# Two-layer hybrid trunk, float32: score matmuls over two PSUM tags, the 32x32 inverses laid out by Vector-engine transposes, output tiles in another pool tag, the second first-layer norm from bn_stats

## Chip, cores and metric

One core of a Trainium2 chip runs the whole program. The metric is device time in microseconds (us) of one execution. The median of three runs of the kernel before is 2872.01 us (2871.85 to 2873.32).

## The reference

256 tokens of width 2048 go through two layers. Each layer normalises the input, multiplies it with one large input projection, runs four token mixers (A to D), projects and gates their outputs, and adds a normalised output projection. Everything is float32. In the code, `ya` is the gated linear attention of `pa`, `yb` the top-k attention of `pb`, `yc` the delta-rule recurrence of `pc` and `yd` the gated token mixer of `pd`.

```python
for l in range(DEPTH):
    h = _rmsnorm(x, norm_pre[l])
    p = h @ w_in[l]
    pa, pb, pc, pd, pm = _split(p, GROUP_COLS)
...
    ys = jnp.stack([ya, yb, yc, yd], axis=2).astype(x.dtype)
    proj = jnp.einsum('bsgw,gwd->bsgd', ys, w_proj[l])
    gates = jax.nn.sigmoid(pm.reshape(bsz, seq, N_BRANCH, D_MODEL).astype(F32))
    merged = jnp.einsum('bsgd,bsgd->bsd', gates, proj.astype(F32)).astype(x.dtype)
    x = x + _rmsnorm(merged @ w_out[l], norm_post[l])
```

The change touches mostly branch C. Its recurrence, per head of 64 channels (16 heads):

```python
def step(state, inp):
    r_t, w_t, k_t, v_t, kk_t, a_t = inp
    sa = jnp.einsum('bhvk,bhk->bhv', state, -kk_t)
    state = (state * w_t[:, :, None, :]
             + sa[..., None] * (kk_t * a_t)[:, :, None, :]
             + v_t[..., None] * k_t[:, :, None, :])
    return state, jnp.einsum('bhvk,bhk->bhv', state, r_t)
```

The kernel computes it in chunks of 64 tokens. Within a chunk it needs the scores between all pairs of tokens (tile `pG`) and the inverse of a unit triangular 64x64 matrix for each head and chunk (tile `TT`), put together from two 32x32 inverses and the block between them.

## The kernel before

**Weights.** `weights` streams the projection matrices with 1 MB DMAs on the SyncE queue (`raw`). Each 128x512 piece is split into a high part `wh` by ScalarE (ACT) and a rest `wl` by VectorE (DVE), three buffers of each. TensorE (PE) makes three products for each piece: high x high, rest x high, high x rest. `product` puts tokens on the PSUM partitions (`mm`, 512 columns wide), `product_cm` puts channels there (`mc`, 256 columns), `product_both` does half of each (`mb`). `shift` is the column at which a split piece starts in its 576-column buffer: 16 by default, 56 in `d_mixer`.

**Stages of a layer.** `pre` transposes the normalised input (`trT`) and splits it into `xT`, ACT the high part and DVE the rest. `small` makes the 280 narrow columns. `c_pair` runs eight times, once for two heads, with the projection of the next pair beside it. `c_solve` makes the inverses, `c_chain` carries the state over four chunks, with `b_index` and `b_pair` (branch B) interleaved. Then come `merge(2)`, branch A, `merge(1)`, `d_mixer`, `merge(0)`, `merge(3)` and `finish`, which makes the layer's output `x` and the next layer's normalised input `o`.

**Order.** A framework schedules the instructions when the program is built, and puts each engine's into a fixed order; an engine runs its own in that order and waits on semaphores. `high_priority` moves instructions ahead in it. Buffers come from pools by tag. A tag with n buffers makes the n+1st tile wait for the readers of the first. PSUM has three tags: `mm` with four banks, `mx` (method `pm`) and `mc` (method `pc`) with two each. The product tiles named `mc` and `mb` lie in tag `mm`.

**Pair scores.** In `c_pair` the two score tiles `pG` come from `pc`, and each is filled by four 64-row matmuls from `kb` and `AR`. GpSimd (POOL) makes `ks` from `kb`, which PE transposes into `pkt`. `pv` transposes the values for `VU`, whose unused half POOL sets to zero in `c_begin`.

**Solve.** `c_solve` runs a forward substitution on DVE in 62 operations on `slv` (128 partitions are 128 blocks of 32x32). The result `X` is written to a DRAM buffer `d2` (shown as `d`), and read back by four DMAs on ACT's queue into `TT`, which has heads and block rows on the partitions. DVE transposes the low blocks of `TT` into `slv` (L645), and PE makes `pzt` and `pet` from them, 64 matmuls of 32x32 each.

**Slots.** `c8` holds six tiles of 16 KB a partition, among them `AR`, `KT`, `VU`, `m2` and `o`. `tt` holds one tile, either `TT` or `npost` (the gain of the output norm). POOL clears a quarter of `TT` twice a layer (L634). The inverse square roots of all norms are a power on POOL (L183).

Of the kernel before, what the change touches and what calls it, by code (L numbers as in the profile page):

```python
# [24 lines left out]
KT = DM // 128  # L25
# [103 lines left out]
class Trunk:  # L129
    def __init__(self, ctx, tc, ins, out, depth=DEPTH, dbg=None):  # L130
        self.ctx, self.tc, self.nc, self.i, self.out, self.depth = ctx, tc, tc.nc, ins, out, depth
        self.dbg = dbg
        self.sb = ctx.enter_context(tc.tile_pool(name="sb", bufs=1))
        self.ps = ctx.enter_context(tc.tile_pool(name="ps", bufs=4, space=PSUM))
        self.dr = ctx.enter_context(tc.tile_pool(name="dr", bufs=1, space=DRAM))
        self.off = 0
        self.BUFS = {"s8": 2, "c8": 6, "tt": 1, "ev": 2, "t2": 8, "s1": 5, "xT": 16, "Y": 2, "c1": 2, "bs": 2, "SP": 2, "zz": 3}

# [226 lines left out]

    def norm(self, x, h):

        ss = self.one([128, 4], "ss", bufs=2)
        for c in range(4):
            junk = self.t("t2", [128, 512], "junk")  # L370
            self.act(junk, x[:, c * 512:(c + 1) * 512], AF.Square, accum_out=ss[:, c:c + 1])
        s1 = self.one([128, 1], "ss1", bufs=2)
        self.nc.vector.tensor_reduce(s1, ss, AX.X, OP.add)
        self.rsqrt(s1, s1, 1.0 / DM, EPS)
        for c in range(4):
            if c % 2:
                self.act(h[:, c], x[:, c * 512:(c + 1) * 512], scale=s1)
            else:
                self.ts(h[:, c], x[:, c * 512:(c + 1) * 512], s1, OP.mult)

    def pre(self, H):

        xT = [self.t("xT", [128, 2, 256], "xT", F32R) for _ in range(KT)]
        for t in range(2):
            for j in range(0, KT, 4):
                ps = self.pm([128, 4, 128], "trT")
                for b in range(4):
                    self.tr(ps[:, b, :], H[t][:, j // 4, b * 128:(b + 1) * 128])
                for b in range(4):
                    s = self.pcol[:, j + b:j + b + 1]  # L390
                    hi, lo = (xT[j + b][:, a, t * 128:(t + 1) * 128] for a in range(2))
                    self.act(hi, ps[:, b, :], scale=s)
                    self.stt(lo, ps[:, b, :], s, hi.bitcast(F32), OP.mult, OP.subtract)
        return xT

    def layer(self, l, H, src):
        nc, i = self.nc, self.i
        self.pcol = self.one([128, NPCOL], "pcol", bufs=2)
        nc.scalar.dma_start(self.pcol, i["pcol"][l])
        self.l = l  # L400
        self.xT = self.pre(H)
        if l == 0:
            self.rope_tables()
        self.small()
        self.c_begin()
        for p in range(8):
            self.c_pair(p)
        self.c_solve()
        ys = {g: [] for g in range(4)}
        self.c_chain(ys[2])  # L410
        self.b_index()
        for p in range(4):
            self.b_pair(p, ys[1])
        self.m2 = [self.t("c8", [128, DM], "m2") for _ in range(2)]
# [26 lines left out]
    def small(self):  # L441
        nc, l = self.nc, self.l
        pa = self.product(self.xT, KT, 280, range(9), range(9))
        s = self.t("ev", [128, 2, 280], "small")
        for t in range(2):
# [50 lines left out]
    def c_pair(self, p):  # L496
# [73 lines left out]
        G = self.t("Y", [128, 2, 4, 128], "G")  # L570
        pg = [self.pc([128, 4, 2, 64], "pG") for _ in range(2)]
        for s in range(4):
# [24 lines left out]
    def c_begin(self):  # L597
        self.AR, self.KT, self.VU, self.bsd = [], [], [], []
        for g in range(2):
            self.AR.append(self.t("c8", [128, 4, 4, 2, 64], "AR"))  # L600
            self.KT.append(self.t("c8", [128, 4, 4, 128], "KT"))
            vu = self.t("c8", [128, 4, 4, 128], "VU")
            self.nc.gpsimd.memset(vu[64:128, :, 0:4:2, :], 0.0)
# [6 lines left out]
    def c_solve(self):  # L610
# [14 lines left out]
        for j in range(31):  # L625
# [3 lines left out]
            self.tt(X[:, 0:j + 1, j + 1:32], X[:, 0:j + 1, j + 1:32], o, OP.add)  # L629
        d2 = self.dr.tile([2, 2, 32, 32, 32], F32, name="d2", bufs=2)  # L630
        nc.scalar.dma_start(d2.rearrange("a b q j t -> (a b q) j t"), X)
        TT = self.t("tt", [128, 32, 64], "TT")
        for h in range(2):
            nc.gpsimd.memset(TT[h * 64 + 32:h * 64 + 64, :, 0:32], 0.0)  # L634
            for qp in range(2):
                r = 64 if qp == 0 else 0
                nc.scalar.dma_start(TT[h * 64:h * 64 + 32, qp * 16:qp * 16 + 16, 32:64],
                                    Gd[r:r + 32, qp * 16:qp * 16 + 16, 0, h * 64 + 32:h * 64 + 64])
            for b in range(2):
                g = h * 64 + b * 32  # L640
                nc.scalar.dma_start(TT[g:g + 32, :, b * 32:(b + 1) * 32], d2[h, b].rearrange("q j t -> j q t"))

        TA, Z = X, M
        for h in range(2):
            nc.vector.transpose(TA[h * 64:h * 64 + 32], TT[h * 64:h * 64 + 32, :, 0:32])  # L645
        lo, hi = ([slice(h * 64 + o, h * 64 + o + 32) for h in range(2)] for o in (0, 32))
# [288 lines left out]
    def d_mixer(self, ys):  # L935
# [25 lines left out]
        for b in range(2):  # L961
            pa = self.product_cm(self.xT, KT, 512, 56)
            u = self.t("ev", [128, 4, 256], "du")
            for j in range(2):
                self.act(u[:, 2 * j:2 * j + 2, :], pa[j], AF.Gelu)
            for j in range(2):
# [8 lines left out]
                self.tt(o, o, w.rearrange("p g t i -> p g (t i)"), OP.mult)  # L975
            pa = self.product_cm(self.xT, KT, 512, 56)
            self.y_slots(ys, 4 * b)
# [34 lines left out]
    def finish(self, src, last):  # L1012
        nc, l = self.nc, self.l
        X = self.load_x(src)
        npost = self.t("tt", [128, DM], "npost")
        nc.scalar.dma_start(npost, self.i["rows"][l, 2304:4352].partition_broadcast(128))
        ss, s1 = [self.one([128, 4], f"osum{t}") for t in range(2)], []
        o = [self.t("c8", [128, 4, 512], "o") for _ in range(2)]
        for d in range(4):
            pa = self.product(self.mT, KT, 512, *((range(8, KT), range(5, KT)) if d == 3 else ()))  # L1020
            for t in range(2):
                junk = self.t("t2", [128, 512], "junk")
                self.act(junk, pa[t], AF.Square, accum_out=ss[t][:, d:d + 1])
                self.tt(o[t][:, d], pa[t], npost[:, d * 512:(d + 1) * 512], OP.mult)
                if d == 3:
# [15 lines left out]
    def run(self):  # L1041
        src = self.i["x"]
        X = self.load_x(src)
        H = [x.rearrange("p (d c) -> p d c", d=4) for x in X]
        self.consts()
        for t in range(2):
            self.norm(X[t], H[t])
        for l in range(self.depth):
# [30 lines left out]
```

## Time and profile before

| | kernel before |
|---|---|
| median of 3 runs | 2872.01 us (2871.85 to 2873.32) |
| profiled execution | 2873.88 us |
| its span in the trace | 2872.1 us |
| PE busy | 2821.7 us (98%) |
| DVE, ACT, POOL busy | 1821.6 (63%), 1484.8 (52%), 174.6 us (6%) |
| mean granted PE clock | 0.995 of full |
| HBM traffic | 185 GB/s over the span |

Busy shares of PE are of pipelined matmuls, whose ends are modelled: a matmul of 128x512 is shown with 0.39 us although the next starts 0.23 us later. So times on PE are read from start to start. The 40-slice view of the page has PE at 9 tenths everywhere but in the first slice and the last. The granted clock reads 1.00 at 2.4 GHz and 0.50 at 1.2 GHz.

### The profile page before, as it was taken

Reading aid. Unit: us, or ns where it says so; the run is one execution under the profiler, and the core shown is the slowest. Engines: PE = TensorE matmul, PEld = TensorE weight load, DVE = VectorE, ACT = ScalarE, POOL = GpSimd, SP = SyncE. Lnnn points to the kernel's source line nnn. Section 1 sums busy time; section 2 is a strip of 40 time slices with the busy share of each in tenths; the row PEclk is TensorE's granted clock in tenths of the full one; section 3 lists DMA queues with packets and bytes.
Section 4 is the critical chain, followed back from the end, with each engine's and each line's share of the span. In section 5 each row is a group of like instructions: output and inputs, shape, how many; then the busy total and the mean of one; then the engine's idle time right before and its main releaser. Section 6 shows DMA issues by size and latency. Waiting matters only on the chain.

```text
span 2872.1 us, 44940 instructions
## 1 busy us (share of the span) xinstructions
PE 2821.7 (98%) x17264; PEld 2442.0 (85%) x17264; DVE 1821.6 (63%) x3319; ACT 1484.8 (52%) x2674; POOL 174.6 (6%) x263
## 2 busy tenths in 40 slices
PE   7999999999999999999989999999999999999998
PEld 6999888887778898888889988898877888988886
DVE  6777857555555655656567779575555556555565
ACT  6455555545444545445565545555554544544454
POOL 1222001000000000000022120110000000000000
PEclk9999999999999999999999999999999999999999
DMA  5555656555455555555555556565545555555554
GB/s 183 182 180 188 192 165 204 179 191 184 166 178 191 189 209 192 191 197 183 184 181 179 181 185 194 158 208 188 197 165 174 183 191 199 197 193 196 191 184 160
DMA packets 100799, 533.56 MB, mean 186 GB/s; under 512 B 30852, under 2 KB 31108, under 8 KB 40742
## 3 DMA queue, kind: packets, MB, share of 16 engines
q1 hardware_dynamic: 68256, 486.96, 48.9%
q10 hardware_dynamic: 26568, 24.85, 3.2%
q0 software_dynamic: 5760, 18.88, 2.0%
q8 instruction: 135, 2.21, 0.3%
q14 instruction: 80, 0.66, 0.1%
HBM read 512.83 MB, written 17.83 MB: 185 GB/s over the span
## 4 chain that ended last, share of the span: by engine, by line
PE 78%; issue 16%; DMA 2%; DVE 2%; ACT 1%; POOL 0%; ACTq 0%; DVEq 0%; POOLq 0%
PE mm L169 49%; PE mc L169 16%; PE mb L169 6%; PE pG L169 1%; DVE wl L157 1%; DMA bs<-bsd 1%; PE pkv L169 1%; PE pW L169 1%; PE pao L169 0%; PE trT L173 0%; PE pY L169 0%; DMA d<-slv 0%; DMA TT<-d 0%; ACT wh L154 0%; PE psc L169 0%
## 5 line engine op out<-in xcount | busy, mean ns | idle before, releaser
L157 DVE TENSOR_TENSOR wl<-raw,wh 128x512 fp32r<-128x512 f32 (+1 forms) x1822 | 1250.4, 689 | 888.6 <-ACT wh L154 884.2
L154 ACT ACTIVATE wh<-raw 128x512 fp32r<-128x512 f32 (+1 forms) x1822 | 1145.7, 630 | 1198.0 <-DVE wl L157 598.3
L169 PE MATMUL mm<-wh,xT 128*128 128x512 f32 (+1 forms) x4216 | 1327.2, 391 | 0.9 <-ACT wh L154 0.9
L169 PEld LDWEIGHTS mm<-wh,xT 128*128 128x128 f32 x4216 | 784.7, 188 | 166.6 <-ACT wh L154 4.8
L169 PE MATMUL mm<-wl,xT 128*128 128x512 f32 (+1 forms) x2108 | 826.9, 392 | 2.7 <-DVE wl L157 2.6
L169 PE MATMUL mc<-xT,wh 128*128 128x256 f32 x3072 | 532.0, 282 | 0.0
L169 PEld LDWEIGHTS mm<-wl,xT 128*128 128x128 f32 x2108 | 395.7, 188 | 92.1 <-DVE wl L157 9.1
L169 PEld LDWEIGHTS mc<-xT,wh 128*128 128x128 f32 x3072 | 447.7, 188 | 5.1
L169 PE MATMUL mc<-xT,wl 128*128 128x256 f32 x1536 | 384.3, 285 | 1.5 <-DVE wl L157 0.9
L169 PE MATMUL mm<-wh,yT 128*128 128x512 f32 x1024 | 321.0, 389 | 0.0
L169 PEld LDWEIGHTS mc<-xT,wl 128*128 128x128 f32 x1536 | 266.0, 188 | 4.9 <-DVE wl L157 3.9
L169 PEld LDWEIGHTS mm<-wh,yT 128*128 128x128 f32 x1024 | 192.1, 188 | 41.3 <-ACT aex L154 1.5
L169 PE MATMUL mm<-wl,yT 128*128 128x512 f32 x512 | 199.4, 389 | 0.0
L169 PE MATMUL mb<-wh,xT 128*128 128x256 f32 x512 | 120.3, 288 | 3.8 <-ACT wh L154 3.8
L169 PEld LDWEIGHTS mm<-wl,yT 128*128 128x128 f32 x512 | 96.1, 188 | 19.9
L169 PE MATMUL mb<-xT,wh 128*128 128x256 f32 x512 | 103.0, 285 | 0.0
L169 PEld LDWEIGHTS mb<-wh,xT 128*128 128x128 f32 x512 | 89.1, 192 | 6.7 <-ACT wh L154 4.2
L169 PEld LDWEIGHTS mb<-xT,wh 128*128 128x128 f32 x512 | 80.1, 192 | 0.8 <-issue 0.5
L169 PE MATMUL mb<-wl,xT 128*128 128x256 f32 x256 | 75.2, 294 | 0.4 <-DVE wl L157 0.4
L169 PE MATMUL mb<-xT,wl 128*128 128x256 f32 x256 | 72.9, 285 | 0.0
L169 PE MATMUL mm<-wown,xT 128*128 128x280 f32 (+1 forms) x204 | 50.0, 387 | 8.1 <-ACT xT L154 5.3
L183 POOL TENSOR_TENSOR orsq<-orsq,mhalf 128x1 f32<-128x1 f32 x4 | 2.4, 588 | 881.0 <-DVE orsq L163 880.9
(280 smaller groups left out, 1924.8 us busy)
## 6 DMA issues: line engine op xcount, KB each, us to landing
raw<-in_w_dram SPq DMA_DIRECT2D x456, 1024.0 KB, 4.8
Gd<-G POOLq DMA_DIRECT2D x32, 256.0 KB, 3.0
Gq<-Gd ACTq DMA_DIRECT2D x8, 1024.0 KB, 5.2
raw<-in_w_dram SPq DMA_DIRECT2D x8, 560.0 KB, 4.0
bsd<-bs POOLq DMA_DIRECT2D x16, 256.0 KB, 4.4
bs<-bsd POOLq DMA_DIRECT2D x16, 256.0 KB, 3.7
x<-in_x_dram ACTq DMA_DIRECT2D x4, 512.0 KB, 5.9
x<-in_x_dram SPq DMA_DIRECT2D x4, 512.0 KB, 7.2
```

Of the source, the lines that this page charges most:

```text
L154: self.nc.scalar.activation(out, in_, f, **kw)
L157: (eng or self.nc.vector).tensor_tensor(out, a, b, op)
L169: self.nc.tensor.matmul(out, lhsT, rhs, start=start, stop=stop, **kw)
L183: self.nc.gpsimd.tensor_tensor(out, out, self.mhalf[:, :n], OP.pow)
```

## The change

- **Pair scores:** one of a pair's two `pG` tiles comes from `pc` and one from `pm`, so that they lie in different PSUM tags.
- **Solve:** DVE transposes `X` twice, straight after the substitution: into `TA` (the scratch tile `slvt`) and into `TT[:, :, 0:32]`, with transposed strides. ACT copies the high blocks from there to `TT[:, :, 32:64]`, and POOL clears their old place afterwards. The DRAM buffer, its write and its four reads are gone.
- **Slots:** `c8` has four buffers, a new tag `vu` has two, for `VU`, `m2` and `o`. `npost` becomes two tiles of 1024 columns in tag `Y`, so `tt` holds `TT` alone.
- **Start:** a 1-element activation (`warm`) stands before the constants. The two norms of the first layer have high priority, and the one of the second token half takes its mean square from `bn_stats` on DVE, not from ACT's squares. The hi and lo splits of `pre` have high priority, and `rope_tables` is called after the product of `small`.
- **d_mixer:** `product_cm` uses the default shift 16 for 56.

```diff
-        self.BUFS = {"s8": 2, "c8": 6, "tt": 1, "ev": 2, "t2": 8, "s1": 5, "xT": 16, "Y": 2, "c1": 2, "bs": 2, "SP": 2, "zz": 3}
+        self.BUFS = {"s8": 2, "c8": 4, "vu": 2, "tt": 1, "ev": 2, "t2": 8, "s1": 5, "xT": 16, "Y": 2, "c1": 2, "bs": 2, "SP": 2, "zz": 3}
...
-    def norm(self, x, h):
+    def norm(self, x, h, stats=False):
...
+        if stats:
+            st, mv = self.t("c1", [128, 4, 6], "nst"), self.t("s1", [128, 2], "nmv")
+            for c in range(4):
+                self.nc.vector.bn_stats(st[:, c, :], x[:, c * 512:(c + 1) * 512])
+            self.nc.vector.bn_aggr(mv, st.rearrange("p b s -> p (b s)"))
+            self.stt(s1, mv[:, 0:1], mv[:, 0:1], mv[:, 1:2], OP.mult, OP.add)
+            self.rsqrt(s1, s1, 1.0, EPS)
...
                 ps = self.pm([128, 4, 128], "trT")
+                with self.tc.high_priority():
...
-        if l == 0:
-            self.rope_tables()
         self.small()
...
-        pg = [self.pc([128, 4, 2, 64], "pG") for _ in range(2)]
+        pg = [f([128, 4, 2, 64], "pG") for f in (self.pc, self.pm)]
...
-            vu = self.t("c8", [128, 4, 4, 128], "VU")
+            vu = self.t("vu", [128, 4, 4, 128], "VU")
...
-        d2 = self.dr.tile([2, 2, 32, 32, 32], F32, name="d2", bufs=2)
-        nc.scalar.dma_start(d2.rearrange("a b q j t -> (a b q) j t"), X)
-        TT = self.t("tt", [128, 32, 64], "TT")
+        TT, TA, Z = self.t("tt", [128, 32, 64], "TT"), tmp, M
+        nc.vector.transpose(TA.rearrange("p q j -> p j q"), X)
+        nc.vector.transpose(TT[:, :, 0:32].rearrange("p q t -> p t q"), X.rearrange("p j t -> p t j"))
         for h in range(2):
-            nc.gpsimd.memset(TT[h * 64 + 32:h * 64 + 64, :, 0:32], 0.0)
+            s = slice(h * 64 + 32, h * 64 + 64)
+            self.act(TT[s, :, 32:64], TT[s, :, 0:32])
+            nc.gpsimd.memset(TT[s, :, 0:32], 0.0)
...
-            for b in range(2):
-                g = h * 64 + b * 32
-                nc.scalar.dma_start(TT[g:g + 32, :, b * 32:(b + 1) * 32], d2[h, b].rearrange("q j t -> j q t"))
-        TA, Z = X, M
-        for h in range(2):
-            nc.vector.transpose(TA[h * 64:h * 64 + 32], TT[h * 64:h * 64 + 32, :, 0:32])
...
-            pa = self.product_cm(self.xT, KT, 512, 56)
+            pa = self.product_cm(self.xT, KT, 512)
...
-        npost = self.t("tt", [128, DM], "npost")
+            npost.append(self.t("Y", [128, 1024], "npost"))
-        o = [self.t("c8", [128, 4, 512], "o") for _ in range(2)]
+        o = [self.t("vu", [128, 4, 512], "o") for _ in range(2)]
...
+        warm = self.t("s1", [128, 1], "warm")
+        self.nc.gpsimd.memset(warm, 0.0)
+        self.act(warm, warm, AF.Square)
...
-            self.norm(X[t], H[t])
+            with self.tc.high_priority():
+                self.norm(X[t], H[t], t == 1)
```

How the built order moves, at three places. On PE, the scores of the first pair of layer 0, in the kernel before (`mc` are products of the next pair):

```order
L169 MATMUL pG<-AR,kb 128x128 x4
L169 MATMUL mc_835<-xT,wh 128x256
L169 MATMUL mc_835<-xT,wl 128x256
L169 MATMUL mc_835<-xT,wh 128x256 x2
L169 MATMUL mc_835<-xT,wl 128x256
L169 MATMUL mc_836<-xT,wh 128x256
L169 MATMUL pG<-AR,kb 128x128 x4
```

and in the changed kernel:

```order
L169 MATMUL mc_836<-xT,wl 128x256
L169 MATMUL pG<-AR,kb 128x128 x8
L173 MATMUL pkt<-cst,ks 128x128 x4
L173 MATMUL pv<-cst,cm 128x128 x2
L169 MATMUL mc_837<-xT,wl 128x256
```

Two groups of four scores with products between them have become one group of eight, with `pkt` and `pv` right behind it.

On DVE, the first transposes after the substitution in layer 0, in the kernel before (`qk` belongs to branch B; the last operation of the substitution stands nine rows ahead of the first transpose):

```order
L157 TENSOR_TENSOR wl<-raw,wh 128x512
L157 TENSOR_TENSOR qk<-ropet 128x8x16 x2
L645 STREAM_TRANSPOSE slv<-TT 32x1024
L157 TENSOR_TENSOR wl<-raw,wh 128x512 x2
L645 STREAM_TRANSPOSE slv<-TT 32x1024
L157 TENSOR_TENSOR wl<-raw,wh 128x512 x6
```

and in the changed kernel:

```order
L157 TENSOR_TENSOR slv<-slv,slvt 128x31
L641 STREAM_TRANSPOSE slvt<-slv 128x32x32
L642 STREAM_TRANSPOSE TT<-slv 128x32x32
L157 TENSOR_TENSOR wl<-raw,wh 128x512 x3
L166 SCALAR_TENSOR_TENSOR by<-po,bg 128x512
```

The two transposes stand right behind the substitution, ahead of the next three splits.

On POOL, the change of layers, in the kernel before (`orsq` and `ss` are inverse roots of norms, `xs` is the output of a layer going to DRAM):

```order
L1035 DMA xs<-x_13545 128x512 x4
L603 MEMSET VU 64x8x128
L604 MEMSET VU 64x8x128
L634 MEMSET TT 32x32x32 x2
L183 TENSOR_TENSOR orsq<-orsq,mhalf 128x1
L183 TENSOR_TENSOR ss_14275<-ss_14275,mhalf 128x1
```

and in the changed kernel:

```order
L183 TENSOR_TENSOR orsq<-orsq,mhalf 128x1
L1043 DMA xs<-x_13542 128x512 x4
L183 TENSOR_TENSOR orsq<-orsq,mhalf 128x1
L183 TENSOR_TENSOR ss_14265<-ss_14265,mhalf 128x1
L1043 DMA xs<-x_13545 128x512 x4
```

The four memsets no longer stand between the layer's output and the two inverse roots.

## Rows read from the trace of the kernel before

**Rows 1.** The page: PE's busy time, and DVE's split group (count, busy us, mean ns).

```profile
PE 2821.7 (98%) x17264; PEld 2442.0 (85%) x17264; DVE 1821.6 (63%) x3319; ACT 1484.8 (52%) x2674; POOL 174.6 (6%) x263
...
L157 DVE TENSOR_TENSOR wl<-raw,wh 128x512 fp32r<-128x512 f32 (+1 forms) x1822 | 1250.4, 689 | 888.6 <-ACT wh L154 884.2
```

**Rows 2.** Timeline of PE around one score group: start us, duration us, operation, count.

```profile
200.41 0.28 PE L169 MATMUL mc<-xT,wh 128*128 128x256 f32 x1
200.61 1.16 PE L169 MATMUL pG<-AR,kb 64*128 64x128 f32 x8
201.70 0.38 PE L169 MATMUL mc<-xT,wh 128*128 128x256 f32 x1
201.92 0.29 PE L169 MATMUL mc<-xT,wl 128*128 128x256 f32 x1
```

**Rows 3.** The tile `ks` in the same pair, instructions that write it.

```profile
L584 POOL TENSOR_TENSOR ks<-kb,P x1: 1431/1431/1431, 198.1 to 198.1; 128x512 f32<-128x512 f32 x1
```

**Rows 4.** Timeline of DVE after the substitution in layer 0.

```profile
361.29 0.21 DVE L157 TENSOR_TENSOR slv<-slv,slvt 128x31 f32<-128x31 f32 x1
...
374.48 1.23 DVE L645 STREAM_TRANSPOSE slv<-TT 32x1024 f32<-32x1024 f32 x1 [6.25 <-DMA TT<-d]
```

**Rows 5.** Timeline of ACT and its queue, same stretch.

```profile
367.89 5.06 ACTq L641 DMA_DIRECT2D TT<-d  x3
373.08 0.63 ACT L154 ACTIVATE wh<-raw 128x512 fp32r<-128x512 f32 x1 [5.97 <-issue]
```

**Rows 6.** Timeline of PE, same stretch, then two groups by form over the span.

```profile
364.90 0.36 PE L169 MATMUL mb<-wh,xT 128*128 128x256 f32 x1
...
370.64 1.03 PE L173 MATMUL pqk<-cst,qk 128*128 128x128 f32 x8
373.76 0.39 PE L169 MATMUL mb<-wh,xT 128*128 128x256 f32 x1 [2.09 <-ACT wh L154]
...
375.77 0.42 PE L169 MATMUL pzt<-slv,TT 32*32 32x32 f32 x4 [1.39 <-DVE slv L645]
...
L169 PE MATMUL mb<-wh,xT 128*128 128x256 f32 x512 | 120.3, 288 | 3.8 <-ACT wh L154 3.8
...
L169 PE MATMUL pzt<-slv,TT 32*32 32x32 f32 x256 | 5.1, 192 | 2.8 <-DVE slv L645 2.8
```

**Rows 7.** Windows behind the two solves: PE busy (count), granted clock, DMA share.

```profile
376.00:381.00 5.00, 4.84 (x26) 0.50 0.12 17
...
1805.00:1808.00 3.00, 3.00 (x16) 0.50 0.33 49
```

**Rows 8.** Timeline of the change of layers.

```profile
1441.38 1.93 POOL L634 MEMSET TT<- 32x1024 f32 x2 [0.86 <-POOL VU L604]
...
1443.99 2.74 DVE L166 SCALAR_TENSOR_TENSOR x<-o,orsq,x 128x512 f32<-128x512 f32 x4 [2.30 <-POOL orsq L183]
...
1447.27 1.94 PE L173 MATMUL trT<-cst,o 128*128 128x128 f32 x8 [9.13 <-DVE o L161]
```

**Rows 9.** Timeline of the start.

```profile
6.29 1.28 ACT L154 ACT_TABLE_LOAD   x1 [6.29 <-DMA x<-in_x_dram]
...
13.64 2.42 DVE L161 TENSOR_SCALAR x<-x,ss 128x512 f32<-128x512 f32 x2 [0.67 <-POOL ss L183]
...
17.56 0.35 ACT L154 ACTIVATE xT<-trT,pcol 128x128 fp32r<-128x128 f32 x1
...
20.46 0.34 DVE L166 SCALAR_TENSOR_TENSOR xT<-trT,pcol,xT 128x128 fp32r<-128x128 f32 x1
```

**Rows 10.** Timeline of PE: 256-column products in `c_pair` (shift 16) and in `d_mixer` (shift 56).

```profile
51.76 0.28 PE L169 MATMUL mc<-xT,wh 128*128 128x256 f32 x1
...
53.47 0.28 PE L169 MATMUL mc<-xT,wh 128*128 128x256 f32 x1
...
1038.74 0.28 PE L169 MATMUL mc<-xT,wh 128*128 128x256 f32 x1
...
1041.89 0.28 PE L169 MATMUL mc<-xT,wh 128*128 128x256 f32 x1
```

More of the change, by code (lines that the diff above doesn't have):

```diff
@@ L364, in load_x @@
         return X
-    def norm(self, x, h):
[L368 to L371, printed above, removed]
-        s1 = self.one([128, 1], "ss1", bufs=2)
-        self.nc.vector.tensor_reduce(s1, ss, AX.X, OP.add)
-        self.rsqrt(s1, s1, 1.0 / DM, EPS)
+    def norm(self, x, h, stats=False):
+        s1 = self.one([128, 1], "ss1", bufs=2)
+        if stats:
[5 more added lines that the diff above has]
+            self.rsqrt(s1, s1, 1.0, EPS)
+        else:
+            ss = self.one([128, 4], "ss", bufs=2)
+            for c in range(4):
+                junk = self.t("t2", [128, 512], "junk")
+                self.act(junk, x[:, c * 512:(c + 1) * 512], AF.Square, accum_out=ss[:, c:c + 1])
+            self.nc.vector.tensor_reduce(s1, ss, AX.X, OP.add)
+            self.rsqrt(s1, s1, 1.0 / DM, EPS)
         for c in range(4):
@@ L386, in pre @@
                 ps = self.pm([128, 4, 128], "trT")
[L387 to L393, printed above, removed]
+                with self.tc.high_priority():
+                    for b in range(4):
+                        self.tr(ps[:, b, :], H[t][:, j // 4, b * 128:(b + 1) * 128])
+                    for b in range(4):
+                        s = self.pcol[:, j + b:j + b + 1]
+                        hi, lo = (xT[j + b][:, a, t * 128:(t + 1) * 128] for a in range(2))
+                        self.act(hi, ps[:, b, :], scale=s)
+                        self.stt(lo, ps[:, b, :], s, hi.bitcast(F32), OP.mult, OP.subtract)
         return xT
@@ L413, in layer @@
             self.b_pair(p, ys[1])
-        self.m2 = [self.t("c8", [128, DM], "m2") for _ in range(2)]
+        self.m2 = [self.t("vu", [128, DM], "m2") for _ in range(2)]
         self.mT = []
@@ L443, in small @@
         pa = self.product(self.xT, KT, 280, range(9), range(9))
+        if l == 0:
+            self.rope_tables()
         s = self.t("ev", [128, 2, 280], "small")
@@ L975, in d_mixer @@
                 self.tt(o, o, w.rearrange("p g t i -> p g (t i)"), OP.mult)
-            pa = self.product_cm(self.xT, KT, 512, 56)
+            pa = self.product_cm(self.xT, KT, 512)
             self.y_slots(ys, 4 * b)
@@ L1014, in finish @@
         X = self.load_x(src)
-        npost = self.t("tt", [128, DM], "npost")
-        nc.scalar.dma_start(npost, self.i["rows"][l, 2304:4352].partition_broadcast(128))
+        npost = []
+        for j in range(2):
+            npost.append(self.t("Y", [128, 1024], "npost"))
+            nc.scalar.dma_start(npost[j], self.i["rows"][l, 2304 + 1024 * j:3328 + 1024 * j].partition_broadcast(128))
         ss, s1 = [self.one([128, 4], f"osum{t}") for t in range(2)], []
-        o = [self.t("c8", [128, 4, 512], "o") for _ in range(2)]
+        o = [self.t("vu", [128, 4, 512], "o") for _ in range(2)]
         for d in range(4):
@@ L1023, in finish @@
                 self.act(junk, pa[t], AF.Square, accum_out=ss[t][:, d:d + 1])
-                self.tt(o[t][:, d], pa[t], npost[:, d * 512:(d + 1) * 512], OP.mult)
+                self.tt(o[t][:, d], pa[t], npost[d // 2][:, (d % 2) * 512:(d % 2) * 512 + 512], OP.mult)
                 if d == 3:
```

## The prediction

> **What bounds the kernel now.** I read the page first: PE is busy for 2821.7 of 2872.1 us, and DVE's largest group, the splits, takes 1250.4 [rows 1]. So only two kinds of edit can pay: those that shorten PE's own list, and those that close one of the few stretches in which PE stands still. I then went through PE's starts for stretches that are longer than their matmuls need, and into the other engines' timelines at each. The edits fall on five places: the start, the small matmuls of `c_pair`, the solve in both layers, the change of layers, and the 256-column products of `d_mixer`.
>
> **Pair scores.** A group of eight matmul records (four score matmuls) starts at 200.61, and PE is back in its products at 201.92. From the product at 200.41 to the one at 201.92 pass 1.51 us, of which two products take 2 x 0.115 [rows 2]; the group costs 1.28. What do eight more in the same group cost? The eight `pqk` records follow one another at (1.03 - 0.28)/7 = 0.107 [rows 6], the `pG` records at (1.16 - 0.28)/7 = 0.126, slow edge included [rows 2]. So 0.86 to 1.0, and joining two groups saves 0.28 to 0.42; I take 0.38, nearer the first, since the edge counts once. Sixteen pairs: **-6.1** (-6.7 to -4.5). A wait that could eat it is `pkt`, now right behind the scores: it needs `ks`, which POOL makes from 198.1 to 199.5 here [rows 3], while PE reached the first score at 200.61. So it is ready 1.1 us before the scores begin, and I cost the wait at nothing. Even if the scores began with `ks`, their group of some 2 us would cover the 1.43 that POOL takes.
>
> **Solve.** In layer 0 the substitution ends at 361.50. Its result comes back to DVE at 374.48 [rows 4], and for most of that time ACT's queue holds the three `TT<-d` reads (5.06 us), with the next split `wh` behind them, at 373.08 after 5.97 idle [rows 5]. PE runs dry: `pqk` should end at 370.64 + 8 x 0.109 = 371.5, the next product starts at 373.76, 2.25 late; three products later `pzt` starts at 375.77, 1.6 late, and 0.4 follows [rows 6]. That is 4.2. Both layers together list 3.8 + 2.8 = 6.6 of idle, of which layer 0 has 2.09 + 1.39 = 3.48 [rows 6]; by the same ratio 8.0 from start to start. Behind the stop the granted clock is 0.50, that is 1.2 GHz, for 5 us in layer 0 and 3 in layer 1 [rows 7]. Half of this, with the edges, is 3.9 more. All of it goes with the reads: -11.9.
>
> What is late next? The changed order has both transposes right behind the substitution on DVE, with `wl` queued behind them, and on ACT two copies `TT<-TT` of 32x1024. A transpose of 32x1024 takes 1.23 [rows 4]. The new ones have 128 partitions of the same 1024 elements and write with a stride. I take 1.23 each, since the elements of a partition are the same, so they end at 361.5 + 2.46 = 363.96. The split behind them ends 0.69 [rows 1] later, at 364.65. In the order `pzt` stands behind the first three products of `mb`, which start at 364.90 [rows 6], so it is asked for at about 365.3, and the split behind `pzt` later still. Neither waits. On ACT the two copies (at 2 x 0.63 [rows 5], twice the elements of a `wh`, 1.2 each) and the four copies of `pzt` lie between two splits, some 4.6 us, while PE has some 2.5 of `pzt` (5.1 in both layers [rows 6]), as much of `pet`, and three pieces of 12 x 0.115 = 1.4 ahead of it; the cover is over 3 us. For what I cannot see I put +0.3: **-11.6** (bounds: -12.5, and with transposes that take twice as long, 4.9 to 366.4, `pzt` 1.1 late in each layer, -9.7). The bound further off is a rival.
>
> The Trainium skill, "VectorE: DVE Perf Modes", in its section "The three transpose paths", gives 311 ns for 128x128 bf16 in blocks of 32x32. Worked out from it, eight such for 1024 columns are an estimate of 2.5 us, about twice the row's 1.23; no run here shows a 128-partition transpose. By that figure the sum below would be 2.0 higher, 2852.2.
>
> **Chain.** In the built order the chain's 64-column matmuls, `pU` and `pS`, stand in five more groups than before. Their edge has no row of its own here; by the edge of the scores, 0.38, that is **+1.9** (0 to +2.2).
>
> **Change of layers.** POOL clears `TT` from 1441.38 to 1443.31, because `npost` has just been read, and only then makes `orsq`; DVE has waited 2.30 for it at 1443.99 and PE starts at 1447.27 after 9.13 us [rows 8]. With the memsets gone from there, which took 1.93, `orsq` is ready about 2 earlier, and the same chain follows: **-2.0** (-2.3 to 0, if something else on POOL is late). The clock, at 1.2 GHz before and after this restart, recovers with the work and moves along.
>
> **Start.** ACT's first square waits for `x` and then for a table load of 1.28 [rows 9]; `warm` loads the table before. Four of ACT's squares go to DVE, which is free. Against this, the four `bn_stats` stand ahead of the first reduction and wait for the second half of `x`; by a split's 0.69 [rows 1] they delay the first transpose by about 0.8. POOL's memsets move off the two `x` scalings, which took 1.21 each beside them [rows 9]. Walked through the order, the first `xT` high part goes from 17.56 to about 15.9 and the first low part from 20.46 [rows 9] to about 16.8. PE's gain is the smaller, and the cosine tables fall into the lockstep of ACT and DVE that follows: **-2.0** (-3.6 to +0.8).
>
> **d_mixer.** Fifteen products in `c_pair` take 53.47 - 51.76 = 1.71 us, 114 ns each; 27 in `d_mixer` 1041.89 - 1038.74 = 3.15, 117 each [rows 10]. If the place of the pieces in their buffers makes that, shift 16 gives up to 2.7 ns on 1536 products, 4.1 us. But it may be the neighbours' traffic. I take half: **-2.0** (-4.1 to +1).
>
> The slots `vu` and `Y`: the tiles that they now share are read long before; nothing.
>
> **Sum.** -6.1 - 11.6 + 1.9 - 2.0 - 2.0 - 2.0 = -21.8. The profiled execution took 2873.88 against a span of 2872.1, and the median is 2872.0. On the profiled execution the sum gives 2852.1, on the median **2850.2**.
>
> **Rivals.**
> 1. *The transposes cost by partition, not by element.* Four times 1.23 is 4.9 each; they end at 371.3, PE waits 5.9 for `pzt` in each layer and the clock falls as before. Against the 11.9 removed stand 11.8 + 3.9: the solve goes from -11.6 to +3.8 and the time is 2865.6. For it: no row has more than 32 partitions or such strides. Against it: the 128-partition elementwise operations on this engine cost what their elements in one partition cost.
> 2. *Slower: strided writes, one element at a time, make a transpose eight times as dear*, 9.8 each. They end at 381.2, PE waits 15.8 in each layer, the sum is -21.8 + 11.6 + 31.6 + 3.9 - 11.9 = +13.4, so 2885.4. The point from which it is slower: PE's wait in a layer over 9 us, that is over 6.5 us for one transpose, 5.3 times the row.
> 3. *The joined scores give nothing*: the records in a group of sixteen run no closer than in two of eight, or `pkt` waits for `ks`. For it: `pm` is also the tag of `pb` and `pv`, so a score tile may wait for a reader. Then 2856.3.
> 4. *Start, change of layers and d_mixer give nothing* (-6.0 falls away): 2856.2.
>
> **How the numbers follow.** My forecast has 0.68, from 2843 to 2855 with its terms at their ends; rivals 3 and 4 together 0.16; rival 1 and cases between it and the forecast 0.11; rival 2 0.04; 0.01 is left. The range of 2842 to 2863 leaves out rivals 1 and 2 and a little at the low end. A change of 0.2% (5.7 us) is about what a measurement can tell from none: faster means below 2866.3. Rival 1 lies just inside, half of it counts as the same: faster 0.90, same 0.06, slower 0.04.
>
> **What would show it.** In the trace after: one PE group of 16 `pG` records a pair, some 2.2 us; two STREAM_TRANSPOSE rows of about 1.2 us right after the substitution, no idle of PE over 0.5 us at `mb` and `pzt`, and a granted clock of 1.00 behind them; `orsq` within 0.7 us of its DVE input at the change of layers, with PE's idle there about 7 us; the first `xT` near 16 us; 256-column products in `d_mixer` at 114 to 116 ns. Wrong would be: transposes over 2.5 us, a clock of 0.50 behind the solve, a gap between the scores and `pkt`, or a start of PE's products later than 18 us.

## The result, and the profile after

| | before | after |
|---|---|---|
| median | 2871.93 us (2871.06 to 2873.32) | 2838.96 us (2837.82 to 2839.60) |
| profiled execution, its span | 2873.88, 2872.1 us | 2839.60, 2837.8 us |
| ratio after / before | | 0.9884, 95% interval 0.9870 to 0.9899 |

The kernel became faster by 33.0 us, where 21.8 was forecast. 2838.96 lies below the range of 2842 to 2863. Set side by side, the starts of PE's stages in the two traces say where the time went (us, between the matmul starts that each row names; the two spans are 34.3 apart):

| stage | before | after | difference |
|---|---|---|---|
| start to the first 256-column product, layer 0 | 43.1 | 39.0 | -4.2 |
| the eight pairs, to the first `mb`, layer 0 and 1 | 271.9, 271.5 | 262.9, 262.5 | -9.0, -9.0 |
| solve, chain, branch B, to the last `mb` | 211.2, 208.9 | 203.8, 204.4 | -7.4, -4.5 |
| `d_mixer`, first to last 256-column product | 93.4, 93.4 | 93.9, 93.9 | +0.5, +0.5 |
| end of that in layer 0 to the first 256-column product of layer 1 | 386.9 | 385.3 | -1.6 |
| all else | | | +0.5 |

The timeline of PE after, around the scores of the first pair (start us, duration us, operation, count); it answers to [rows 2]:

```profile
81.05 0.28 PE L169 MATMUL mc<-xT,wl 128*128 128x256 f32 x1
81.25 1.16 PE L169 MATMUL pG<-AR,kb 64*128 64x128 f32 x16
82.34 0.66 PE L173 MATMUL pkt<-cst,ks 128*128 128x128 f32 x4
82.84 0.38 PE L173 MATMUL pv<-cst,cm 128*128 128x128 f32 x2
```

Sixteen records take 1.16 us, the time that eight took before. One head's operands lie on partitions 0 to 63, the other's on 64 to 127 (two 64-row halves of TensorE's array, below "halves"), and the loop in `c_pair` takes the heads in turn. Once the group runs, the records start 7 and 105 ns apart by turns; in the group of eight of [rows 2] they start 112 ns apart. This is the row that the prediction did not foresee.

The solve in layer 0 after, on DVE, on ACT, on PE, and PE's window behind it (busy, count, granted clock, DMA share); it answers to [rows 4 to 7]:

```profile
348.33 2.10 DVE L641 STREAM_TRANSPOSE slvt<-slv 128x1024 f32<-128x1024 f32 x1
350.27 1.99 DVE L642 STREAM_TRANSPOSE TT<-slv 128x1024 f32<-128x1024 f32 x1
...
352.30 2.13 ACT L154 ACTIVATE TT<-TT 32x1024 f32<-32x1024 f32 x2
...
352.20 2.21 PE L169 MATMUL pzt<-slvt,TT 32*32 32x32 f32 x128
...
352.00:357.00 5.00, 5.00 (x153) 1.00 0.01 3
```

The transposes take 2.0 to 2.1 us, not 1.23, and PE waits for neither: `pzt` has no row of idle time ahead of it, and the granted clock stays at 1.00, 2.4 GHz.

The change of layers after; it answers to [rows 8]:

```profile
1421.25 0.56 POOL L183 TENSOR_TENSOR orsq<-orsq,mhalf 128x1 f32<-128x1 f32 x1 [2.81 <-DVE orsq L163]
...
1421.85 2.74 DVE L166 SCALAR_TENSOR_TENSOR x<-o,orsq,x 128x512 f32<-128x512 f32 x4 [0.32 <-POOL orsq L183]
...
1425.13 1.94 PE L173 MATMUL trT<-cst,o 128*128 128x128 f32 x8 [7.16 <-DVE o L161]
```

POOL now stands ready and waits 2.81 us for DVE; DVE's wait for POOL's `orsq` is 0.32 where it was 2.30. PE stands still for 7.16 us, 9.13 before [rows 8]. (In the view of 40 slices before, the slice with this stop is the one inner slice at 8 tenths for PE.)

The start after, ACT and DVE; it answers to [rows 9]:

```profile
1.67 1.28 ACT L154 ACT_TABLE_LOAD   x1 [1.67 <-PEq L1079]
...
15.35 0.34 ACT L154 ACTIVATE xT<-trT,pcol 128x128 fp32r<-128x128 f32 x1
...
16.29 0.34 DVE L166 SCALAR_TENSOR_TENSOR xT<-trT,pcol,xT 128x128 fp32r<-128x128 f32 x1
```

The table is loaded while `x` is on its way, and the first high and low parts come 2.2 and 4.2 us earlier.

PE's waits after (us in total, times, longest):

```profile
PE mc L169 <- DVE wl L157: 3.2, 8, 0.5
PE mm L169 <- ACT wh L154: 2.4, 4, 0.8
```

and before:

```profile
PE mm L169 <- ACT wh L154: 0.9, 2, 0.7
PE mc L169 <- DVE wl L157: 0.9, 2, 0.5
```

Some of the gain went again in these small new waits; the experiments below come back to them.

### The profile page after: what moved, and what is told of

It reads as the page before. It is cut to its first block, busy times and chain, and to the rows that moved or that the text cites. A ratio compares the mean times of both kernels' runs of the same rounds, so it can differ in the third digit from the quotient of the medians.

```text
span 2837.8 us, 44972 instructions
## 1 busy us (share of the span) xinstructions
PE 2798.4 (99%) x17264; PEld 2422.0 (85%) x17264; DVE 1820.6 (64%) x3324; ACT 1483.4 (52%) x2671; POOL 180.1 (6%) x264
## 4 chain that ended last, share of the span: by engine, by line
PE 79%; issue 16%; DVE 2%; ACT 1%; DMA 1%; ACTq 0%; POOL 0%; DVEq 0%; SPq 0%; POOLq 0%
PE mm L169 50%; PE mc L169 15%; PE mb L169 7%; DVE wl L157 1%; PE pG L169 1%; PE pkv L169 1%; PE pW L169 1%; PE pY L169 1%; PE trT L173 0%; PE pao L169 0%; ACT wh L154 0%; DMA raw<-in_w_dram 0%; PE po L169 0%; PE plg L169 0%; PE psc L169 0%
```

## The experiments

Each run stands beside runs of the kernel before on the same chip. "Saved" is the difference of the two medians. The changed kernel saved 33.0.

| run | median us | saved | ratio, 95% interval |
|---|---|---|---|
| one tag again | 2854.03 | 18.2 | 0.9937 (0.9922 to 0.9952) |
| two tags, halves apart | 2850.03 | 22.2 | 0.9921 (0.9906 to 0.9936) |
| kernel before with two tags alone | 2857.61 | 14.6 | 0.9950 (0.9933 to 0.9966) |
| old solve | 2850.89 | 21.3 | 0.9926 (0.9911 to 0.9941) |
| old start | 2844.03 | 28.0 | 0.9904 (0.9889 to 0.9918) |
| no early table load, no bn_stats | 2844.77 | 28.4 | 0.9899 (0.9884 to 0.9914) |
| old slots | 2840.61 | 31.4 | 0.9890 (0.9875 to 0.9905) |
| shift 56 | 2838.17 | 33.8 | 0.9883 (0.9868 to 0.9898) |
| `pkv` in two tags | 2835.60 | 36.4 | 0.9873 (0.9857 to 0.9890) |
| `pinv` on ACT | 2837.03 | 36.1 | 0.9873 (0.9856 to 0.9889) |
| both of these | 2832.36 | 40.8 | 0.9859 (0.9845 to 0.9874) |
| score reads on POOL's queue | 2836.01 | 36.0 | 0.9874 (0.9861 to 0.9888) |
| all three | 2827.15 | 44.9 | 0.9844 (0.9831 to 0.9858) |

The intervals are some 4 us wide to each side; differences of 1 to 3 us between two rows rest on the traces beside them. One more run, the transposes in plain order, was made once and stands below alone.

**One tag again.**

```diff
-        pg = [f([128, 4, 2, 64], "pG") for f in (self.pc, self.pm)]
+        pg = [self.pc([128, 4, 2, 64], "pG") for _ in range(2)]
```

> The changed kernel with one edit undone: both score tiles of a pair come from the same PSUM tag again. The trace of the changed kernel shows 16 pG records in one group of 1.16 us, the time that 8 took before, with starts alternating 7 and 105 ns. Theory (two tags let the two heads of a pair, on different row halves of the array, run side by side): the stage from the first pair to branch B gets back what it gained, 18 us in the two layers, and the kernel takes about 2857 us. Rival (only the group's edge is saved, 0.38 us in 16 pairs): 2845 us. If the gain of the c stage comes from somewhere else (buffers, alignment): 2839 to 2841 us.

Measured: 14.8 us of the 33.0 are lost. That is nearer to the theory's 18 than to the 6 of the edge. PE's timeline of this run shows the old pattern, two groups with products between them:

```profile
141.45 1.16 PE L169 MATMUL pG<-AR,kb 64*128 64x128 f32 x8
...
143.09 1.16 PE L169 MATMUL pG<-AR,kb 64*128 64x128 f32 x8
```

The two small waits are back near their old 0.9 in this run, so they came with the joined scores:

```profile
PE mm L169 <- ACT wh L154: 1.0, 2, 0.5
PE mc L169 <- DVE wl L157: 0.8, 2, 0.5
```

**Two tags, halves apart.**

```diff
-        for s in range(4):
-            q = 2 * (s % 2) + s // 2
-            for h in range(2):
+        for h in range(2):
+            for s in range(4):
+                q = 2 * (s % 2) + s // 2
```

> The changed kernel with its two tags, but the eight score matmuls of a pair written head by head, so that four of one row half are followed by four of the other. The group stays one group, its edge is saved as before. Theory (it is the alternation of row halves that pays): starts come every 112 ns again, the group takes about 2.0 us in place of 1.16, 16 x 0.85 = 13.6 us more, 2852.5 us. Rival (what pays is the joining, or the two banks): no change, 2839 us.

Measured: 10.8 us are lost, where the theory had 13.6. The group is still one group, but it takes longer:

```profile
82.09 1.71 PE L169 MATMUL pG<-AR,kb 64*128 64x128 f32 x16
```

The starts of its records say why it is 1.71 and not 2.0. They come 112 ns apart at its start and its end; in the middle, where the first half gives way to the second, three times two records start 4 to 6 ns apart. So the alternation of halves is worth at least 10.8, and at most 4.0 of the 14.8 are left for the joining, since a part of the overlap is still in this run.

**The kernel before with two tags alone.** The edit is the first one, turned round, on the kernel before.

> The kernel before with one edit alone: the two score tiles from two PSUM tags. Theory (side by side in the array): 18 us less than before, 2854 us, and groups of 16 records in 1.16 us. Rival (the gain needs the other edits, by the order that they make): less than 8 us, 2864 us or more.

Measured: 14.6 us less. The groups of 16 in 1.16 us are there too. The gain needs none of the other edits, and undoing it costs as much as doing it gives.

**Old solve.**

```diff
-        nc.vector.transpose(TA.rearrange("p q j -> p j q"), X)
-        nc.vector.transpose(TT[:, :, 0:32].rearrange("p q t -> p t q"), X.rearrange("p j t -> p t j"))
+        d2 = self.dr.tile([2, 2, 32, 32, 32], F32, name="d2", bufs=2)
+        nc.scalar.dma_start(d2.rearrange("a b q j t -> (a b q) j t"), X)
...
+                nc.scalar.dma_start(TT[g:g + 32, :, b * 32:(b + 1) * 32], d2[h, b].rearrange("q j t -> j q t"))
```

> The changed kernel with the old solve: the result of the substitution goes through DRAM and back by four DMAs on ACT's queue, and two transposes of 32x1024 follow. Theory (the round trip cost two stops of PE in each layer and the half clock behind them, 11.9 us, and the new solve adds next to nothing): 2849 to 2851 us, with PE idle near pzt and a granted clock of 0.50 behind it. Rival (most of the gain of that stage comes from the order of the chain and branch B around it): 2843 us or less.

Measured: 11.7 us are lost, as expected. PE's timeline and window in layer 0 of this run:

```profile
363.23 0.31 PE L169 MATMUL pzt<-slv,TT 32*32 32x32 f32 x4 [4.02 <-DVE slv L654]
...
365.00:368.00 3.00, 3.00 (x17) 0.57 0.05 14
```

One wait of 4.02 us stands where the kernel before had two of 2.09 and 1.39 [rows 6], and the granted clock behind it is 0.57 in the mean of these 3 us, at the level of 1.2 GHz for most of them. In layer 1 that wait is 4.33. The round trip costs here what it cost before, in another order around it.

**Old start.** All edits of the start are undone:

```diff
-        warm = self.t("s1", [128, 1], "warm")
...
-            with self.tc.high_priority():
-                self.norm(X[t], H[t], t == 1)
+            self.norm(X[t], H[t])
```

and with them the high priority in `pre` and the place of `rope_tables`.

> The changed kernel with the old start: no early activation, the norms and the splits of the transposed input at normal priority, both norms from ACT's squares, the cosine tables ahead of the narrow product. Theory (the start gains what the first 256-column product shows, 43.11 against 38.95 us): 4 us more, 2843 us. Rival (the gain there is the moved POOL memsets, which stay): 2840 us.

Measured: 5.0 us are lost. The first 256-column product starts at 40.9 us against 39.0 here, and between 39.0 and 40.2 in the other runs with the new start. So 0.7 to 2 us are lost at the start itself, and the rest further on: 1.0 and 2.1 in the pairs of the two layers, 0.7 and 1.2 in the stage behind them, while the change of layers is 0.9 shorter.

**No early table load, no bn_stats.**

```diff
-                self.norm(X[t], H[t], t == 1)
+                self.norm(X[t], H[t])
```

and the three lines of `warm` are gone; the priorities stay.

> The changed kernel without the early activation and without bn_stats: both norms of the first layer from ACT's squares, still with high priority, as the splits of the transposed input. Undoing the whole start cost 5 us, of which the trace shows 2 before the first 256-column product and 3 later, in the c stages. Theory (the early table load and DVE's share of the squares make the gain at the start, the priorities the rest): 2 us more, 2841 us. Rival (the priorities make it all): 2839 us.

Measured: 4.6 us are lost, as much as with the whole old start. The priorities and the moved tables give nothing that shows. ACT's timeline of this run has the table load behind `x` again, and the first high part 1.9 us later than after:

```profile
5.95 1.28 ACT L154 ACT_TABLE_LOAD   x1 [5.95 <-DMA x<-in_x_dram]
...
17.22 0.35 ACT L154 ACTIVATE xT<-trT,pcol 128x128 fp32r<-128x128 f32 x1
```

Here too up to 1.8 are lost before the first 256-column product and some 3 later. The scheduler puts the whole program in order, so an edit at the start also changes rows of later stages. In this run and in the one with the old start, PE waits 1.6 us at `mb` for `wl`, and the changed kernel has no such row; what the rest of the 3 us is was not separated.

**Old slots.**

```diff
-        self.BUFS = {"s8": 2, "c8": 4, "vu": 2, "tt": 1, "ev": 2, "t2": 8, "s1": 5, "xT": 16, "Y": 2, "c1": 2, "bs": 2, "SP": 2, "zz": 3}
+        self.BUFS = {"s8": 2, "c8": 6, "tt": 1, "ev": 2, "t2": 8, "s1": 5, "xT": 16, "Y": 2, "c1": 2, "bs": 2, "SP": 2, "zz": 3}
...
+        npost = self.t("tt", [128, DM], "npost")
```

> The changed kernel with the old slots: six buffers of one tag for AR, KT, VU, m2 and o, and the output norm's gain in the slot of TT. Theory (the change of layers gains 1.6 us because POOL's memsets no longer stand ahead of the inverse roots): 2840.5 us, if the memset of TT, which stands later in the new solve, goes back ahead of the roots; with the new solve it may not, and then the slots alone give nothing, 2839 us. Either way under 2843 us.

Measured: 1.6 us, which the intervals do not tell from nothing. What the trace loses is at the start: POOL's memsets of `VU` stand beside DVE's second pair of `x` scalings again, which take 0.89 us each in place of 0.48, PE waits 1.8 us for `xT` from DVE (0.3 after), and the first 256-column product starts at 40.2. At the change of layers it loses nothing: the stretch from the end of `d_mixer` to the first 256-column product of layer 1 takes 385.1 us, as after (385.3); with the old solve and the new slots it takes 383.9. PE's idle there is 7.2 and 7.1; in the kernel before with two tags alone, which has neither edit, it is 9.1. So either edit alone frees POOL at the change of layers: new slots, since `TT` no longer waits for `npost`, or the new solve, since its memsets stand behind ACT's copies, much later.

**Shift 56.**

```diff
-            pa = self.product_cm(self.xT, KT, 512)
+            pa = self.product_cm(self.xT, KT, 512, 56)
```

> The changed kernel with the pieces of d_mixer at column 56 again. In the trace of the changed kernel the 256-column products of that stage take 117.8 ns, before 116.7. Theory A (the place in the buffer makes it): back to 116.7, 1536 x 1.1 ns = 1.7 us less, 2837.3 us. Theory B (the place of the buffers, which moved with the slots, or the neighbours make it): no change, 2839 us. The prediction's term (column 16 is faster): 2 us more, 2841 us.

Measured: 0.8 us more saved than the changed kernel, not to be told from it by the intervals. The traces agree with theory A: 18 products of `d_mixer` in the changed kernel take 1002.34 - 1000.22 = 2.12 us, 117.8 ns each,

```profile
1000.22 0.28 PE L169 MATMUL mc<-xT,wl 128*128 128x256 f32 x1
...
1002.34 0.28 PE L169 MATMUL mc<-xT,wl 128*128 128x256 f32 x1
```

and with column 56 the same 18 take 1003.02 - 1000.92 = 2.10 us, 116.7 ns each, as before [rows 10]:

```profile
1000.92 0.28 PE L169 MATMUL mc<-xT,wl 128*128 128x256 f32 x1
...
1003.02 0.28 PE L169 MATMUL mc<-xT,wl 128*128 128x256 f32 x1
```

The stage from its first product to its last is 93.4 us at 56 and 93.9 at 16: over its 768 products 0.65 ns each. With the old slots and column 16 it is 93.9 too, so the place of the buffers, which moved with the slots, does not make it.

**The transposes in plain order.**

```diff
-        nc.vector.transpose(TA.rearrange("p q j -> p j q"), X)
-        nc.vector.transpose(TT[:, :, 0:32].rearrange("p q t -> p t q"), X.rearrange("p j t -> p t j"))
+        nc.vector.transpose(TA, X)
+        nc.vector.transpose(TT[:, :, 0:32], X)
```

> The changed kernel with both transposes of the solve in plain order, block by block, without the transposed strides; the layout that the inverses need is left out, the amount of work is the same. In the trace of the changed kernel they take 2.10 and 1.99 us, where a transpose of 32x1024 took 1.23 before. Theory A (the strides of the write cost the difference): 1.2 to 1.3 us each. Theory B (four times the partitions cost it): 2.0 us each. The time of the whole stays within 1 us of 2839 either way, since no engine waits for them.

Measured: 2838.4 us, one run. DVE's groups of this run (busy us, mean ns):

```profile
L641 DVE STREAM_TRANSPOSE slvt<-slv 128x1024 f32<-128x1024 f32 x2 | 2.5, 1246 | 0.1
L642 DVE STREAM_TRANSPOSE TT<-slv 128x1024 f32<-128x1024 f32 x2 | 2.4, 1202 | 0.0
```

Theory A holds. With 128 partitions a transpose costs what it cost with 32 [rows 4]; the transposed strides cost the other 0.8.

**`pkv` in two tags.** The same edit in `a_head`:

```diff
-            pk = [self.pc([128, 256], "pkv") for _ in range(2)]
+            pk = [f([128, 256], "pkv") for f in (self.pc, self.pm)]
```

> The changed kernel with the same edit at a second place: the two key-value products of a chunk in branch A, which also lie on the two row halves, get one tile from each of the two tags. In the built order three of the four stand together now and one alone, before two together and two alone. Theory (halves side by side, and a group's edge less for each of 16 heads): 16 x 0.2 to 0.4, 3 to 6 us in the 8 heads of both layers at most, 2833 to 2836 us. Rival (the third is alone on its half, only an edge is saved, 8 x 0.3): 2836.5 us. Against it: the second tag is also that of the transposed queries, and a wait there would cost PE something.

Measured: 3.4 us more saved, at the low end of the theory. The stretch from the last `mb` to the first product of `d_mixer`, in which branch A lies, is 1.7 and 1.6 us shorter in the two layers. PE's timeline of the first head, in the changed kernel:

```profile
693.04 0.70 PE L169 MATMUL pkv<-qkv 64*128 64x256 f32 x4
...
697.53 0.70 PE L169 MATMUL pkv<-qkv 64*128 64x256 f32 x2
...
699.71 0.70 PE L169 MATMUL pkv<-qkv 64*128 64x256 f32 x2
```

and in this run:

```profile
694.58 1.13 PE L169 MATMUL pkv<-qkv 64*128 64x256 f32 x6
...
700.83 0.70 PE L169 MATMUL pkv<-qkv 64*128 64x256 f32 x2
```

Six and two records take 1.83 us where four, two and two took 2.10, and one edge is gone. The first fence also shows four records, two of each half, in the 0.70 us of two of one half.

**`pinv` on ACT.**

```diff
-        nc.vector.reciprocal(pinv.rearrange("p (c t) -> p c t", c=4), P[:, :, 1:65])
+        self.act(pinv, sg, AF.Exp, scale=DECAY)
```

> The changed kernel with pinv, the inverse of the decay P, made as an exponential on ACT (256 columns, some 0.42 us as P itself) in place of a reciprocal on DVE, which takes 1.75 us in each of 16 pairs. From the groups' costs the joined scores should save 16 x 1.3 = 21 us, and undoing them gave back 15. Theory (6 us of it are lost again, because DVE's list in a pair is now the longer one: the split behind the reciprocal comes 0.6 us late in 12 pairs, 0.2 before): the waits of PE at mc for wl go, 5 us less, 2834 us. Rival (the wait moves to the next split, or to ACT, which gets 0.4 us more a pair): 2838 to 2840 us.

Measured: 3.1 us more saved, of the 5 expected. PE's waits of this run:

```profile
PE mm L169 <- ACT wh L154: 4.4, 4, 1.9
```

The wait of `mc` for `wl`, 3.2 us after, has no row any more: DVE's longer list was its cause. But the wait of `mm` for `wh` grew from 2.4 to 4.4. Its two long ones, 1.5 and 1.9, lie at the end of the pairs, where ACT issues the reads of the scores. Theory and rival each have a part.

**Both of these.** The two diffs above together.

> Both follow-ups together on the changed kernel: pinv on ACT, and the key-value products of branch A in tiles from two tags, which alone gave 2835.6 us. They lie in different stages, so their gains should add: 3.4 + 5 us less, 2830.5 us, if the pinv edit gives its 5; 2835 us if it gives nothing.

Measured: 40.8 saved, 7.8 more than the changed kernel; the two add up, 3.4 and 3.1, and a little more. ACT's timeline in layer 1 of this run shows what holds the next split:

```profile
1683.61 4.56 ACTq L649 DMA_DIRECT2D TT<-Gd  x4
1688.28 0.63 ACT L154 ACTIVATE wh<-raw 128x512 fp32r<-128x512 f32 x1 [4.06 <-DMA TT<-Gd]
```

**Score reads on POOL's queue**, in the combination and in the changed kernel:

```diff
-                    nc.scalar.dma_start(M[g:g + 16], ...
+                    nc.gpsimd.dma_start(M[g:g + 16], ...
-                nc.scalar.dma_start(TT[h * 64:h * 64 + 32, qp * 16:qp * 16 + 16, 32:64],
+                nc.gpsimd.dma_start(TT[h * 64:h * 64 + 32, qp * 16:qp * 16 + 16, 32:64],
```

> The combination (pinv on ACT, key-value products in two tags; 2832.4 us) with the twelve reads of the scores into slv and TT on POOL's queue, where before they are on ACT's. In its trace ACT's next split stands 4.1 us behind four TT<-Gd issues of 4.56 us, and PE waits over 2 us for it at the end of the c stage in each layer. Theory (these issues on ACT's queue give back what the joined scores and the pinv edit gain): the waits of PE for wh there go, 3 to 4 us less, 2828.5 us. Rival (POOL's queue lands the data so much later that the solve ends too late for pzt, or the substitution falls behind): 2833 us or more.

> The changed kernel with the same move alone. Its trace shows PE waiting 0.9 us in each layer for a split behind such reads. Theory: 1.8 us less, 2837.2 us. Rival (a late solve): 2840 us or more.

Measured: 3.0 us more saved in the changed kernel, 4.1 more in the combination, 44.9 in all. PE's waits for `wh` at `mm`, first in the combination, then in the changed kernel with this move:

```profile
PE mm L169 <- ACT wh L154: 1.4, 2, 0.9
```

```profile
PE mm L169 <- ACT wh L154: 1.1, 2, 0.7
```

They were 4.9 in the combination without the move and 2.4 after. So the issues on ACT's queue were the second place where time was given back. Of the 3.0 us in the changed kernel these waits are 1.3; the rest was not followed up. Whether the move, or `pinv` on ACT, would pay without the joined scores was not run. With all three edits the kernel takes 2827.15 us and beats both kernels of this study.

## Why the prediction was wrong, point by point

**Pair scores: -6.1 forecast, -14.8 by undoing it, -14.6 alone.** 8.7 of the miss of 11.2 us are here. The prediction's step that failed is the answer to "what do eight more in the same group cost?" I read 0.86 to 1.0 us for them, from pitches of `pqk` and `pG` [rows 2, 6]. In those rows all records follow one another on the same rows of the array: in the kernel before, each group holds the four score matmuls of one head, that is of one row half. The joined group alternates the heads, and two matmuls on different halves start 7 ns apart. Eight more cost nothing: 1.16 us for sixteen as for eight. The run with the halves apart shows that this, not the edge (what a group loses at its two ends), is at least 10.8 of the 14.8 us. At most 4.0 are left for the edge, where I had 6.1. I had the mechanism of the edit (one group in place of two) and not its larger part. The trace of the kernel before could have told it. Its PE timeline, in the heads of branch A:

```profile
713.63 0.70 PE L169 MATMUL pkv<-qkv 64*128 64x256 f32 x4
...
718.12 0.70 PE L169 MATMUL pkv<-qkv 64*128 64x256 f32 x2
```

Four records, two of each half, take the 0.70 us of two of one half; the four start in two pairs, 7 ns apart in each. I read the pitches of the scores and not this row.

The Trainium skill says it in "TensorE: Matmul & The Clock Gate", section "Part 3: Packing small matmuls — row/col tiling": matmuls on different tiles of the array run at the same time and start about 4 ns apart. By that rule the term of the scores would have come out larger. The trace after agrees in kind: two records start 6 to 7 ns apart here, not 4, and 16 take 1.16 us. How much of it is had depends on the order of issue: with the halves apart the same 16 take 1.71 us.

**What was given back.** From the groups' times the scores should have saved more: before, two groups of 1.28 us with their edges and at least 0.6 for `pkt` and `pv`; after, 1.8 to 1.9 for all in one stretch. That is an estimate of 1.3 to 1.4 us less a pair, some 21 in 16 pairs. 14.8 came out. Of the remaining 6 the two waits named above, DVE's split behind the 1.75 us reciprocal and ACT's split behind the score reads, list 3.8: 3.2 and 2.4 after, 0.8 and 1.0 with one tag again. The runs that go after them gave 3.1 and 3.0 alone. That the whole 6 went there is not shown. In the forecast I named `ks` as the wait that might eat the gain; it did not, `pkt` follows the scores without a gap.

**Solve and chain: -11.6 + 1.9 forecast, -11.7 by undoing the solve.** The price of the stalls and of their half clock held: PE does not wait, the clock stays at 1.00. The term that was mis-sized is the transpose, 2.10 and 1.99 for 1.23: elements of a partition was right, strides were free was wrong. The walk had not shown that this costs nothing: it let `pzt` wait for both transposes, and with these times both end at 361.5 + 4.1 = 365.6, 0.3 after `pzt` is asked for at 365.3. But `pzt` needs only the first. In the run with the score reads on POOL's queue it starts 0.16 us after the first ends and 1.58 before the second does:

```profile
353.28 2.09 DVE L641 STREAM_TRANSPOSE slvt<-slv 128x1024 f32<-128x1024 f32 x1
355.19 1.92 DVE L642 STREAM_TRANSPOSE TT<-slv 128x1024 f32<-128x1024 f32 x1
...
355.53 2.21 PE L169 MATMUL pzt<-slvt,TT 32*32 32x32 f32 x128
```

In the changed kernel the first ends at 350.43 and `pzt` starts at 352.20, so 1.8 us were to spare. The estimate of 2.5 by the Trainium skill ("VectorE: DVE Perf Modes", section "The three transpose paths") was nearer to the 2.0 to 2.1 than my row, but by luck: in plain order the same transposes take 1.20 to 1.25, half of it, and the rest is the strides. The chain's +1.9 does not show in the stage's sum; it was not tested alone. Rivals 1 and 2, transposes that cost four or eight times, are out: they cost 1.6 to 1.7 times.

**Change of layers: -2.0 forecast.** The trace gives -1.6 over the stretch and 1.97 in PE's wait there. The mechanism was as told: POOL's memsets stood ahead of `orsq`. The runs added that either of two edits is enough for it.

**Start: -2.0 forecast, -5.0 by undoing it.** At the start itself it was about right in the trace, where 0.7 to 2 us go with it, most of them with the early table load and `bn_stats`. Of the 4.2 in the table above the new slots give some 1.2 more, by POOL's memsets, which I had put under the start. The other 3 of the 5.0 lie in the pairs of both layers and the stage behind them, where I looked for nothing. How the order there follows from the start stays open.

**`d_mixer`: -2.0 forecast, about +1 in the trace.** The sign was wrong. The products became slower at column 16, 117.8 for 116.7 ns, and went back at 56. I had taken the difference between two stages [rows 10] for one between two columns; the column did not make it, and what made it stays open.

**The sum.** Undoing the edits one by one costs 14.8 + 11.7 + 5.0 + 1.6 - 0.8 = 32.3 of 33.0 us. So within the intervals the edits add, though the sum holds the 1.6 of the change of layers nowhere: either of two edits keeps it, and the 1.6 of the old slots stands at the start in their trace. The miss is that of the terms: scores -8.7, start -3.0, solve and chain -2.0, change of layers +0.4, `d_mixer` +2.8. Start, change of layers (by the trace) and `d_mixer` together gave 5.0 + 1.6 - 0.8 = 5.8 for the 6.0 forecast, but that is luck: the start gave 3.0 too much and `d_mixer` had the wrong sign. The range was too high because its low end took each term's own bound, and the scores went past theirs, -14.8 for -6.7, as the start did, -5.0 for -3.6. I had excluded that a matmul could cost nothing.

## What to carry to other kernels

Before pricing a matmul by the pitch of its neighbours, look which rows of the array each uses: small matmuls on different row halves, alternated, cost half here (sixteen in 1.16 us, as eight of one half). What keeps them apart can be a pool of buffers, and the built order of the other kernel shows it, if one asks not only how many stand together but which. When PE's list gets shorter in a stage, read at once which engine's list is now the longest there; here 0.2 to 0.4 us a pair went back, much of it to a reciprocal on one engine and to a queue of reads on another, until both were moved.

## What the runs showed of the hardware that was not expected

- Two 64-row matmuls of 64x128 on different halves of the array start 6 to 7 ns apart, the next two 105 ns later, where two on the same half start 112 ns apart. Even written half by half, some records in the middle of the group of 16 start 4 to 6 ns apart, and it takes 1.71 us, not the 2.0 expected.
- A DVE transpose of 1024 elements in a partition takes 1.20 to 1.25 us on 32 and on 128 partitions, and 2.0 to 2.1 with transposed strides.
- The column at which a weight piece starts in its buffer moved the pitch of the 256-column products by some 1 ns in a stretch of `d_mixer` (117.8 at 16, 116.7 at 56), 0.65 over the whole stage; in the pairs, at 16 as well, it lies at 114 in the stretch of [rows 10].
